# Another place in SBUF for the combined blocks, the activations and the raw weights, and a larger descriptor reserve for GpSimd's DMAs

## The chip, the cores and the metric

One Trainium2 chip, one core of it. The metric is the device time of one execution of the whole program in microseconds, as the median of several runs. TensorE, VectorE, ScalarE and GpSimd stand as PE, DVE, ACT and POOL in the profile; SyncE (SP) issues most of the DMAs, POOL issues some, and PEld is TensorE's weight load.

## What is computed

One decoder block on 1024 tokens of width 1024 in float32: half a SwiGLU feed forward, a mixer of two linear attentions with gates, half a SwiGLU feed forward, a final norm.

```python
def swiglu(h, w_gate, w_up, w_down):
    return (jax.nn.silu(h @ w_gate) * (h @ w_up)) @ w_down

h = h + FFN_RES * swiglu(rms_norm(h, ffn1_norm[layer]), ...)      # 1024 -> 2816 -> 1024
h = h + hybrid_mixer(rms_norm(h, mix_norm[layer]), ...)
h = h + FFN_RES * swiglu(rms_norm(h, ffn2_norm[layer]), ...)
return rms_norm(h, final_norm)
```

The mixer is a projection of h, gated linear attention with 4 heads, Gated DeltaNet with 8 heads in its chunked form (a triangular solve for each chunk of 64 tokens), gates on both, their sum, and an output projection.

## The kernel before

**Number format.** Every weight and activation of the large products is split into a high part and a low part (`wh`, `wl` for weights, `xh`, `xl` for activations). A product is three matmuls: `wh` with `xl`, `wl` with `xh`, `wh` with `xh`. Nearly all of them are 128x128 weights on 512 columns. A weight half arrives by an SP DMA in a tile `raw` (or `sr`), ACT casts it to `wh` (L119, L125) and DVE subtracts to get `wl` (L120, L126).

**Stages.** The first feed forward, the mixer, the second feed forward run one after the other. In a feed forward, gate and up projections are done for pairs of units by a Strassen scheme (`strassen`, matmuls at L367): seven products of 12 matmuls each. Four products read the split activations `xh`, `xl`; the other three read combined blocks of them, `t2h`, `t2l`, `t3h`, `t3l`, `t4h`, `t4l`, which are made once by `sums_own`. There are 20 such Strassen calls in each feed forward, that is 20 x 84 matmuls, 20 x 36 of them on combined blocks. The down projection (`down`, L573) uses the same six tiles anew, and `c11`, `c21`, `c22`, `wt`, for two of its four chunks, and `xn` tiles for the other two. The first and last rows of it go through `accumulate` (L138) with activations in `ah`, `al` and (last rows) in `t2h`, `t2l`; for the last rows the weights are kept in `t3h`, `t3l`, `t4h`, `t4l` by `hold`. The output projection of the mixer holds its second half of weights in the same way. The mixer has combined blocks of its own, from pool `mx`, for its Strassen calls (psum tag `m`).

**The triangular solves.** In the DeltaNet part, POOL inverts the blocks of one head while PE works on projections and on the head before. For each head POOL issues four DMAs of `em` to `l_d` (L920), four back to `lt` (L923), runs 31 pairs of multiply and subtract (L930, L933), then writes the result with four DMAs `x_d<-xp` of 1024 pieces each (L937) and one of `xt` (L938), and reads it back with eight DMAs to `xb` and `yb` (L949, L950). PE's first matmul on `xb` is at L986.

**Order.** The program is written in a tile language whose scheduler sets the order on each engine by priorities and its own view of when things are ready; each engine then runs its list in order. Tiles come from pools. A pool takes space from the low end of what is free, or from the high end with `side="right"`, when it is opened, and gives it back when it closes; a tile with a tag uses the slots of its tag in turn. The pools concerned:

```python
wp = ctx.enter_context(tc.tile_pool(name="wp", bufs=4))             # raw, wh, wl
...
raw = stage() if stage else wp.tile([P, 512], F32, name="raw", tag="raw", bufs=2)
...
hp = pool(st, "h1")       # the residual
tp = pool(st, "t1")       # everything else of the first feed forward
...
nc = _bacc.Bacc("TRN2", target_bir_lowering=False, num_devices=1, dynamic_dma_scratch_size=2048)
```

The last number is the bytes of each SBUF partition, from address 0, that are kept for the descriptors of DMAs which POOL issues.

Of the kernel before, what the change touches and what calls it, by code (L numbers as in the profile page):

```python
# [48 lines left out]
def tile_macaron_hybrid(  # L49
# [21 lines left out]
    xn = ctx.enter_context(tc.tile_pool(name="xn", bufs=1))  # L71
    wp = ctx.enter_context(tc.tile_pool(name="wp", bufs=4))

    nc.scalar.preload_act_table_set("sqrt_and_others")
# [234 lines left out]

    def strassen_products(tp, xs, tmp, corner, raws, place=bank, pool_steps=3):  # L310
        comb = {}
# [111 lines left out]

    def ffn(h, xs, wg, wu, wd, tp, ysc, first, last, pre, steps, after):
        def act_tiles():
            return [tp.tile([P, T], F32R, name=n, tag=n, bufs=2) for n in ("ah", "al")]

        def gate_up(j):
# [8 lines left out]
            if j == 0:  # L437
                b = tp.tile([P, T], F32, name="al", tag="al", bufs=2)
# [16 lines left out]
        def raws():  # L455
            return ([wp.tile([P, 512], F32, name="raw", tag="raw", bufs=2) for _ in range(2)] +
                    [stage() for _ in range(2)])
# [3 lines left out]

        sums_own, sums_inplace, strassen = strassen_products(tp, xs, weight_sum, weight_sum, raws, pool_steps=2)

# [61 lines left out]
        def chunk_ops(c):  # L525
            names = ("b11", "b21", "t2", "t3", "t1", "t4", "b22")
            res = {}
            for i, n in enumerate(names):
# [3 lines left out]
                elif i < 6:  # L532
                    m = ("t2h", "t2l", "t3h", "t3l", "t4h", "t4l")[i]
                    t = tp.tile([P, 4, 512], F32R, name=m, tag=m)
                    res[n] = [[t[:, 2 * p + k] for k in range(2)] for p in range(2)]
# [5 lines left out]
        def prepare(c, ops, first=None):  # L541
            parts = [first] if first else []
            for k in range(len(parts), 2):
                ss = [tp.tile([P, T], F32, name=n, tag=n, bufs=2) for n in (("ah", "al") if k and c else ("s", "s"))]
                for i in range(2):
# [5 lines left out]
        def down(u, ops, h0, h1, steps):  # L551
            r1 = wp.tile([P, 512], F32, name="raw", tag="raw", bufs=2)
            r2 = tp.tile([P, 512], F32, name="sr", tag="sr", bufs=2)
# [58 lines left out]
        with tc.issue_after(done[0]):  # L612
            at = [tp.tile([P, T], F32, name="ah", tag="ah", bufs=2) for _ in range(2)]
            for i in range(4):
                sums_inplace(i, lambda eng: at[i % 2][:, (LO, HI)[i // 2]])
# [22 lines left out]
        for n in ("t2h", "t2l"):  # L638
            t = tp.tile([P, 4, 512], F32R, name=n, tag=n).rearrange("p (j a) t -> p j (a t)", j=2)
            kept.append([t[:, k] for k in range(2)])  # L640
# [8 lines left out]
        ns = norm_space(tp)  # L649
        held = hold(wd, prev[0], tp)  # L650
        for seg in last:
# [9 lines left out]

    with ExitStack() as st:
        hp = pool(st, "h1")
        tp = pool(st, "t1")
# [25 lines left out]
        def between(seg, ns):  # L690
            steps = norm_steps(h, seg, P_MX, xs2, ns)
            if seg[0] == 0:
# [5 lines left out]
                       steps=steps)  # L698
        ffn(h, xs, g1, u1, d1, tp, ysc, FIRST, HALVES, begin1, None, between)
        with tc.high_priority(offset=-4000):  # L700
# [3 lines left out]
    with ExitStack() as st:  # L704
        with ExitStack() as stm:
            ys, h = mixer(stm, st, tc, pool, start, xs2, load_unit, dense, ptile, bank, rsqrt_newton, split, new_x,
                           accumulate, block_units(OBLOCKS), dram, pr, ident, ones, cst, eye, wlr, win,
                           wout, y_d, h_d, sqrt_table, strassen_products, wp, psum, divide, recent, pinned, run)
# [4 lines left out]
        held = hold(wout, units, tp)  # L713
        ysc = tp.tile([P, T], F32, name="ysc", tag="ysc")
# [18 lines left out]

        ffn(h, xs, g2, u2, d2, tp, ysc, HALVES, LAST, None, steps, finish)


def mixer(st, sto, tc, pool, start, xs, load_unit, dense, ptile, bank, rsqrt_newton, split, new_x, accumulate,
          ounits, dram, pr, ident, ones, cst, eye, wlr, win, wout, y_d, h_d, sqrt_table, strassen_products, wp, psum, divide, recent, pinned, run):
    nc = tc.nc
# [512 lines left out]
    for i in range(8):  # L1252
# [32 lines left out]
    sums_own, sums_inplace, strassen = strassen_products(  # L1285
        mx, xs, lambda: wp.tile([P, 512], F32, name="raw", tag="raw", bufs=2),
        lambda: wp.tile([P, 512], F32, name="raw", tag="raw", bufs=2),
        lambda: [mx.tile([P, 512], F32, name="sr", tag="sr", bufs=4) for _ in range(4)],
# [78 lines left out]
    sqrt_table()  # L1367
    return ys, h

# [85 lines left out]
```

## Time and profile before

| what | us |
|---|---|
| runs of the kernel | 2658.49, 2653.29, 2659.28 |
| median | 2658.49 |
| the profiled execution's own time | 2661.61 |
| its span, first to last instruction | 2659.8 |
| PE busy in the span | 2505.2 (94%) |
| DVE busy | 1872.5 (70%) |
| POOL busy | 1177.3 (44%) |
| ACT busy | 1069.3 (40%) |

Matmuls overlap each other in the records: a row gives the time from a matmul's start to its modelled end, and the next one starts before that. What a row of matmuls takes is read from the starts. The stages by the clock of the span: first feed forward 0 to 730 us (gate and up from 95 to 465, down to 671, last rows to 720), DeltaNet heads to about 1320, gated linear attention and gates to 1850, output projection to 1960, second feed forward to the end (gate and up from 2010 to 2390).

### The profile page before, as it was taken

How to read it: one execution, taken by the hardware profiler on the slowest of the kernel's cores; microseconds unless marked ns; L12 is line 12 of the kernel's file. 1: busy time of each engine (PE TensorE's matmuls, PEld its weight loads, DVE VectorE, ACT ScalarE, POOL GpSimd, SP SyncE). 2: the span in 40 equal slices, each digit the busy share in tenths (PEclk: the TensorE clock that was granted, in tenths of full speed). 3: DMA queues.
4: the chain of work that ended last, by engine and by line, in shares of the span. 5: the costliest groups of instructions: out<-in, count | busy, mean ns of one | idle time of the engine just before them, and what ended most of it. 6: DMA issues, size and time to landing. Idle time of an engine off the chain costs nothing.

```text
span 2659.8 us, 32713 instructions
## 1 busy us (share of the span) xinstructions
PE 2505.2 (94%) x11656; PEld 2020.1 (76%) x11656; DVE 1872.5 (70%) x2907; ACT 1069.3 (40%) x1847; POOL 1177.3 (44%) x1312
## 2 busy tenths in 40 slices
PE   7899999899986999999989999999989999998998
PEld 6788888667865777777767787878768888886677
DVE  8755555999685777886686766767586555558996
ACT  5333334333352444444354544535243333343331
POOL 4544444654227667776352222121154444446531
PEclk9999999999998999999999999999999999999999
DMA  3222221322221222212211212112312222213222
GB/s 116 76 68 88 87 87 58 117 80 84 106 84 48 60 64 60 60 44 56 60 55 40 84 36 84 60 60 91 119 32 80 76 79 84 91 60 112 80 87 79
DMA packets 93602, 199.03 MB, mean 75 GB/s; under 512 B 12248, under 2 KB 17112, under 8 KB 93440
## 3 DMA queue, kind: packets, MB, share of 16 engines
q1 hardware_dynamic: 82576, 175.64, 20.3%
q0 software_dynamic: 8704, 18.89, 2.7%
q10 hardware_dynamic: 2160, 2.43, 0.3%
q8 instruction: 91, 1.49, 0.2%
q14 instruction: 71, 0.58, 0.1%
HBM read 158.73 MB, written 38.17 MB: 74 GB/s over the span
## 4 chain that ended last, share of the span: by engine, by line
PE 66%; DVE 15%; POOL 5%; ACT 5%; issue 4%; DMA 2%; DVEq 0%; POOLq 0%; ACTq 0%
PE q L367 28%; PE ps L138 13%; PE m L367 10%; PE q L573 6%; DVE wl L126 2%; PE q L986 2%; DVE xl L126 1%; POOL itmp L930 1%; POOL xp L933 1%; DVE ha L578 1%; DVE h L578 1%; DMA s<-a_d 1%; ACT L803 1%; PE q L908 1%; DVE c L378 1%
## 5 line engine op out<-in xcount | busy, mean ns | idle before, releaser
L126 DVE TENSOR_TENSOR wl<-raw,wh 128x512 fp32r<-128x512 f32 x244 | 199.7, 819 | 173.1 <-ACT wh L125 171.6
L138 PE MATMUL ps<-xl,wh 128*128 128x512 f32 (+2 forms) x736 | 258.3, 410 | 22.9 <-ACT wh L119 8.0
L126 DVE TENSOR_TENSOR wl<-sr,wh 128x512 fp32r<-128x512 f32 x232 | 203.5, 878 | 78.6 <-ACT wh L125 78.2
L138 PE MATMUL ps<-xh,wh 128*128 128x512 f32 (+2 forms) x736 | 255.2, 406 | 0.0
L138 PE MATMUL ps<-xh,wl 128*128 128x512 f32 (+2 forms) x736 | 254.8, 404 | 0.1
L367 PE MATMUL q<-xl,wh 128*128 128x512 f32 x640 | 249.6, 390 | 0.3 <-ACT c L373 0.3
L367 PE MATMUL q<-xh,wl 128*128 128x512 f32 x640 | 249.7, 390 | 0.0
L367 PE MATMUL q<-xh,wh 128*128 128x512 f32 x640 | 249.6, 390 | 0.0
L125 ACT CAST wh<-sr 128x512 fp32r<-128x512 f32 x232 | 143.7, 619 | 243.4 <-PE q L573 61.8
L472 POOL TENSOR_TENSOR s<-s,ysc 128x512 f32<-128x512 f32 x80 | 112.5, 1417 | 247.2 <-ACT s L471 247.2
L125 ACT CAST wh<-raw 128x512 fp32r<-128x512 f32 x244 | 145.0, 594 | 176.5 <-PE q L367 98.3
L138 PEld LDWEIGHTS ps<-xl,wh 128*128 128x128 f32 (+1 forms) x736 | 138.8, 193 | 54.2 <-DVE xl L238 8.9
L355 POOL TENSOR_TENSOR raw<-sr 128x512 f32<-128x512 f32 x20 | 26.6, 1328 | 331.0 <-DMA sr<-in_win 269.8
L138 PEld LDWEIGHTS ps<-xh,wh 128*128 128x128 f32 (+1 forms) x736 | 138.7, 193 | 24.2 <-issue 1.0
L138 PEld LDWEIGHTS ps<-xh,wl 128*128 128x128 f32 (+1 forms) x736 | 138.9, 192 | 24.0 <-issue 0.9
L378 DVE TENSOR_TENSOR c<-c,q 128x512 f32<-128x512 f32 x120 | 82.4, 687 | 84.2 <-PE q L367 84.0
L367 PEld LDWEIGHTS q<-xl,wh 128*128 128x128 f32 x640 | 120.2, 188 | 26.8 <-issue 0.7
L367 PEld LDWEIGHTS q<-xh,wl 128*128 128x128 f32 x640 | 120.2, 188 | 25.5
L367 PEld LDWEIGHTS q<-xh,wh 128*128 128x128 f32 x640 | 120.2, 188 | 25.2
L373 ACT COPY c<-q 128x512 f32<-128x512 f32 x120 | 70.4, 587 | 162.2 <-PE q L367 161.8
L930 POOL TENSOR_TENSOR itmp<-lt,xp 128x112 f32<-128x112 f32 (+29 forms) x248 | 116.1, 468 | 36.1 <-DMA lt<-l_d 17.3
L933 POOL TENSOR_TENSOR xp<-xp,itmp 128x112 f32<-128x112 f32 (+29 forms) x248 | 120.0, 484 | 19.4
(490 smaller groups left out, 6848.7 us busy)
## 6 DMA issues: line engine op xcount, KB each, us to landing
sr<-in_win SPq DMA_DIRECT2D x80, 256.0 KB, 2.6
a_d<-s SPq DMA_DIRECT2D x36, 512.0 KB, 3.6
raw<-in_win SPq DMA_DIRECT2D x66, 256.0 KB, 2.6
raw<-in_d SPq DMA_DIRECT2D x56, 256.0 KB, 2.7
raw<-in_g SPq DMA_DIRECT2D x48, 256.0 KB, 2.6
s<-a_d SPq DMA_DIRECT2D x24, 512.0 KB, 4.1
sr<-in_u SPq DMA_DIRECT2D x44, 256.0 KB, 3.0
raw<-in_u SPq DMA_DIRECT2D x44, 256.0 KB, 2.6
```

Of the source, the lines that this page charges most:

```text
L125: a = nc.scalar.copy(out=hi, in_=src)
L126: b = (eng or nc.vector).tensor_sub(out=lo, in0=src, in1=hi.bitcast(F32))
L138: mm = nc.tensor.matmul(out=ps[:m, sl], lhsT=w[:, :m], rhs=x[:, sl], start=(i == 0 and a == 0), stop=(i == n - 1 and a == 2))
L367: nc.tensor.matmul(out=ps, lhsT=p[:, c], rhs=q, start=(first and k == 0 and a == 0), stop=(k == 3 and a == 2), skip_group_check=not first)
L373: marks[0] = nc.scalar.copy(out=t, in_=ps).ins
L378: marks[1] = nc.vector.tensor_add(out=t, in0=t, in1=ps).ins
L472: nc.gpsimd.tensor_mul(out=s, in0=s, in1=y)
L573: nc.tensor.matmul(out=ps, lhsT=p[:, c], rhs=q, start=(first and k == 0 and a == 0), stop=(k == 1 and a == 2), skip_group_check=not first)
L578: nc.vector.scalar_tensor_tensor(out=hd[:, sl], in0=ps, scalar=0.5, in1=hd[:, sl], op0=ALU.mult, op1=ALU.add)
L930: inv_eng.tensor_tensor(out=tv, in0=lp[:, j, j + 1:].unsqueeze(2).broadcast_to([P, r, m]), in1=xp[:, j, :m].unsqueeze(1).broadcast_to([P, ...
L933: inv_eng.tensor_tensor(out=xv, in0=xv, in1=tv, op=ALU.subtract)
L986: nc.tensor.matmul(out=q[:, c], lhsT=lhs[:, c], rhs=rhs[:, c], start=True, stop=True)
```

## The change

It is one edit in three parts. (1) A pool `rp` at the high end of SBUF holds the `raw` tiles, which were at the front of `wp`. (2) A pool `q1` (in the second feed forward `q2`) is opened ahead of the residual's pool and holds `t2h` to `t4l`, `ah` and `al`; the pool `t1` (`t2`) keeps the rest. (3) The reserve for POOL's DMAs grows from 2048 to 8192 bytes. No tile is added, none changes its size or its number of slots, and no instruction's work changes.

```diff
+    rp = ctx.enter_context(tc.tile_pool(name="rp", bufs=2, side="right"))
...
-            raw = stage() if stage else wp.tile([P, 512], F32, name="raw", tag="raw", bufs=2)
+            raw = stage() if stage else rp.tile([P, 512], F32, name="raw", tag="raw", bufs=2)
...
-    def strassen_products(tp, xs, tmp, corner, raws, place=bank, pool_steps=3):
+    def strassen_products(tp, xs, tmp, corner, raws, place=bank, pool_steps=3, tq=None):
...
-                comb[c] = [tp.tile([P, 4, 512], F32R, name=c + p, tag=c + p) for p in "hl"]
+                comb[c] = [(tq or tp).tile([P, 4, 512], F32R, name=c + p, tag=c + p) for p in "hl"]
...
-            return [tp.tile([P, T], F32R, name=n, tag=n, bufs=2) for n in ("ah", "al")]
+            return [tq.tile([P, T], F32R, name=n, tag=n, bufs=2) for n in ("ah", "al")]
...
-        held = hold(wd, prev[0], tp)
+        held = hold(wd, prev[0], tq)
...
     with ExitStack() as st:
+        tq = pool(st, "q1")
         hp = pool(st, "h1")
         tp = pool(st, "t1")
...
     stl.close()
+    tq = pool(sto, "q2")
     hp = pool(sto, "h2")
...
-    nc = _bacc.Bacc("TRN2", target_bir_lowering=False, num_devices=1, dynamic_dma_scratch_size=2048)
+    nc = _bacc.Bacc("TRN2", target_bir_lowering=False, num_devices=1, dynamic_dma_scratch_size=8192)
```

What lies where, in bytes from the start of a partition, as the built programs place it (a partition ends at 229,376):

| tiles | before | after |
|---|---|---|
| reserve for POOL's descriptors | 0 to 2,048 | 0 to 8,192 |
| `xh0` to `xl7` | 3,840 to 69,376 | 9,984 to 75,520 |
| `raw` | 69,376 to 73,472 | 225,248 to 229,344 |
| `wh`, `wl` | 73,472 to 89,856 | 75,520 to 91,904 |
| mixer's `t2h` to `t4l` (`mx`) | 89,856 to 139,008 | 91,904 to 141,056 |
| residual `h` | 89,856 to 122,624 | 157,440 to 190,208 |
| first feed forward: `t2h`, `t2l`, `t3h`, `t3l`, `t4h`, `t4l`, 8,192 each | 157,568 to 206,720 | 100,096 to 149,248 |
| second: `t3h`, `t3l`, `t4h`, `t4l` | 145,280 to 178,048 | 91,904 to 124,672 |
| second: `t2h`, `t2l` | 190,336 to 206,720 | 132,864 to 149,248 |
| `al` (two), first / second | 149,376 / 182,144, 8,192 long | 91,904 / 124,672 |
| `ah` (two), both | 206,720 to 214,912 | 149,248 to 157,440 |
| `s`, `sr`, `wt`, `c11` to `c22`, `ysc` | 122,624 to 149,248 or so | 190,208 to 216,832 or so |

**The order on the engines** is the same in both feed forwards and from about 1320 us on. It differs in the DeltaNet heads. Lines after L71 have moved by one to three, and buffer numbers differ. On PE, ahead of the first matmul on `xb` of the first head (`n` and `xb` are its inputs, `acc` the next values to be transposed, `ps` a projection), before:

```order
L138 MATMUL ps<-xl_5419,wh 128x512 x2
L138 MATMUL ps<-xh_5418,wl 128x512 x2
L138 MATMUL ps<-xh_5418,wh 128x512 x2
L138 MATMUL ps<-xl_5424,wh 128x512 x2
L138 MATMUL ps<-xh_5423,wl 128x512 x2
L986 MATMUL q<-xb,n_5770 128x128 x4
L138 MATMUL ps<-xh_5423,wh 128x512 x2
L138 MATMUL ps<-xl_5429,wh 128x512 x2
```

and with the change:

```order
L139 MATMUL ps<-xl_5425,wh 128x512 x2
L139 MATMUL ps<-xh_5424,wl 128x512 x2
L139 MATMUL ps<-xh_5424,wh 128x512 x2
L139 MATMUL ps<-xl_5430,wh 128x512 x2
L139 MATMUL ps<-xh_5429,wl 128x512 x2
L139 MATMUL ps<-xh_5429,wh 128x512 x2
L139 MATMUL ps<-xl_5435,wh 128x512
L989 MATMUL q<-xb,n_5777 128x128 x4
L139 MATMUL ps<-xl_5435,wh 128x512
```

Three projection matmuls that stood behind the matmul on `xb` now stand ahead of it (`xh_5423,wh` x2 and one of `xl_5429,wh`).

On PE again, some 60 us earlier: the transposes of the first head's keys (`q<-cs,kq`), those of the decay and beta rows (`q<-cs,yi`), and the first of the products of keys and queries (`q<-kq`), before:

```order
L1234 MATMUL q<-cs,yi 128x128
L138 MATMUL ps<-xl_5429,wh 128x512
L1234 MATMUL q<-cs,yi 128x128 x2
L882 MATMUL q<-cs,kq_5782 128x128 x8
L138 MATMUL ps<-xl_5429,wh 128x512
L138 MATMUL ps<-xh_5428,wl 128x512 x2
L138 MATMUL ps<-xh_5428,wh 128x512 x2
L138 MATMUL ps<-xl_5434,wh 128x512
L1234 MATMUL q<-cs,yi 128x128
```

and with the change:

```order
L139 MATMUL ps<-xl_5450,wh 128x512
L1237 MATMUL q<-cs,yi 128x128 x2
L885 MATMUL q<-cs,kq_5789 128x128 x2
L1237 MATMUL q<-cs,yi 128x128
L885 MATMUL q<-cs,kq_5789 128x128 x6
L1237 MATMUL q<-cs,yi 128x128
L139 MATMUL ps<-xl_5450,wh 128x512
L911 MATMUL q<-kq_5789 128x256 x4
```

The key transposes have moved back behind 18 projection matmuls and stand next to the `q<-kq` products, which stay at nearly the same place (three rows of projection later).

## Rows read from the trace of the kernel before

**Rows 1.** Windows by stage: stretch, length, busy us (instructions), granted clock, DMA share, GB/s.

```profile
core 0: us, PE busy (x) PEld busy (x) DVE busy (x) ACT busy (x) POOL busy (x), PEclk, DMA share, GB/s
...
320.00:440.00 120.00, 120.00 (x524) 98.08 (x523) 67.22 (x92) 45.43 (x79) 52.28 (x37) 1.00 0.23 73
...
520.00:600.00 80.00, 71.98 (x299) 54.56 (x298) 76.62 (x104) 29.65 (x55) 48.46 (x45) 1.00 0.23 73
...
800.00:860.00 60.00, 37.94 (x183) 30.84 (x181) 31.85 (x68) 11.59 (x21) 43.02 (x84) 0.83 0.19 50
860.00:925.00 65.00, 62.60 (x345) 50.03 (x344) 48.84 (x106) 27.87 (x54) 41.65 (x84) 1.00 0.23 64
...
2240.00:2360.00 120.00, 120.00 (x524) 98.16 (x523) 67.27 (x92) 44.69 (x77) 51.91 (x36) 1.00 0.25 82
```

**Rows 2.** Chain of work that ended last: start us, us, what.

```profile
95.12 369.59 PE q L367 x1608
...
2010.03 380.35 PE q L367 x1656
```

**Rows 3.** Timeline of PE, first feed forward: start us, us, engine line op tiles.

```profile
299.82 0.39 PE L367 MATMUL q<-xl,wh 128*128 128x512 f32 x1
...
301.86 0.40 PE L367 MATMUL q<-t2l,wh 128*128 128x512 f32 x1
...
304.65 0.40 PE L367 MATMUL q<-t3l,wh 128*128 128x512 f32 x1
```

**Rows 4.** Timeline of PE, mixer, 24 matmuls on its combined blocks.

```profile
1601.19 0.39 PE L367 MATMUL m<-t2l,wh 128*128 128x512 f32 x1
...
1603.91 0.39 PE L367 MATMUL m<-t3l,wh 128*128 128x512 f32 x1
...
1606.63 0.39 PE L367 MATMUL m<-xl,wh 128*128 128x512 f32 x1
```

**Rows 5.** PE by shape: 96 to 464, 672 to 693, 1895 to 1930 us (busy us, mean ns).

```profile
L367 PE MATMUL q<-xh,wh 128*128 128x512 f32 x307 | 119.7, 390 | 0.0
...
L367 PE MATMUL q<-t3h,wh 128*128 128x512 f32 x76 | 30.0, 395 | 0.0
...
L138 PE MATMUL ps<-ah,t3h 128*128 128x512 f32 x8 | 2.5, 389 | 0.0
...
L138 PE MATMUL ps<-xh,t3h 128*128 128x512 f32 x32 | 10.0, 395 | 0.0
...
L138 PE MATMUL ps<-xh,wh 128*128 128x512 f32 x10 | 3.1, 390 | 0.0
```

**Rows 6.** PE's waits, 500 to 640 us: total, times, longest.

```profile
PE q L573 <- DVE ha L578: 12.9, 14, 2.6
```

**Rows 7.** Timeline of POOL, first head; in brackets the idle time before.

```profile
831.32 0.83 POOL L937 DMA_DIRECT2D x_d<-xp  x1
834.37 0.78 POOL L937 DMA_DIRECT2D x_d<-xp  x1 [2.21 <-issue]
837.25 0.77 POOL L937 DMA_DIRECT2D x_d<-xp  x1 [2.10 <-issue]
840.12 0.78 POOL L937 DMA_DIRECT2D x_d<-xp  x1 [2.10 <-issue]
...
843.33 0.58 POOL L949 DMA_DIRECT2D xb<-x_d  x1 [0.70 <-DMA x_d<-xp]
```

**Rows 8.** POOL's waits, whole span, and DMA issues of the page's view: KB, us to landing.

```profile
POOL x_d L937 <- issue: 60.1, 24, 4.3
...
x_d<-xp POOLq DMA_DIRECT2D x32, 32.0 KB, 2.6
```

**Rows 9.** PE's waits, 730 to 1320 us.

```profile
PE q L986 <- DMA xb<-x_d: 25.6, 4, 20.9
PE q L908 <- DVE h L805: 6.7, 6, 1.3
```

**Rows 10.** Casts and subtractions of weights by tile read, whole span (512 columns).

```profile
L125 ACT CAST wh<-raw 128x512 fp32r<-128x512 f32 x212 | 131.9, 622 | 157.4 <-PE q L367 98.3 <-PE q L573 39.0 <-PE ps L138 7.4
...
L125 ACT CAST wh<-sr 128x512 fp32r<-128x512 f32 x232 | 143.7, 619 | 243.4 <-PE q L573 61.8 <-PE q L367 60.0 <-PE m L367 44.5
```

More of the change, by code (lines that the diff above doesn't have):

```diff
@@ L422, in strassen_products, with ffn @@
         return sums_own, sums_inplace, strassen
-    def ffn(h, xs, wg, wu, wd, tp, ysc, first, last, pre, steps, after):
+    def ffn(h, xs, wg, wu, wd, tq, tp, ysc, first, last, pre, steps, after):
         def act_tiles():
-            return [tp.tile([P, T], F32R, name=n, tag=n, bufs=2) for n in ("ah", "al")]
+            return [tq.tile([P, T], F32R, name=n, tag=n, bufs=2) for n in ("ah", "al")]
         def gate_up(j):
@@ L437, in gate_up @@
             if j == 0:
-                b = tp.tile([P, T], F32, name="al", tag="al", bufs=2)
+                b = tq.tile([P, T], F32, name="al", tag="al", bufs=2)
                 with tc.high_priority(offset=400):
@@ L455, in raws @@
         def raws():
-            return ([wp.tile([P, 512], F32, name="raw", tag="raw", bufs=2) for _ in range(2)] +
+            return ([rp.tile([P, 512], F32, name="raw", tag="raw", bufs=2) for _ in range(2)] +
                     [stage() for _ in range(2)])
@@ L460, in weight_sum @@
             return tp.tile([P, 512], F32, name="wt", tag="wt", bufs=2)
-        sums_own, sums_inplace, strassen = strassen_products(tp, xs, weight_sum, weight_sum, raws, pool_steps=2)
+        sums_own, sums_inplace, strassen = strassen_products(tp, xs, weight_sum, weight_sum, raws, pool_steps=2, tq=tq)
         def gate_up2(j):
@@ L533, in chunk_ops @@
                     m = ("t2h", "t2l", "t3h", "t3l", "t4h", "t4l")[i]
-                    t = tp.tile([P, 4, 512], F32R, name=m, tag=m)
+                    t = tq.tile([P, 4, 512], F32R, name=m, tag=m)
                     res[n] = [[t[:, 2 * p + k] for k in range(2)] for p in range(2)]
@@ L543, in prepare @@
             for k in range(len(parts), 2):
-                ss = [tp.tile([P, T], F32, name=n, tag=n, bufs=2) for n in (("ah", "al") if k and c else ("s", "s"))]
+                ss = [p.tile([P, T], F32, name=n, tag=n, bufs=2)
+                      for p, n in (((tq, "ah"), (tq, "al")) if k and c else ((tp, "s"), (tp, "s")))]
                 for i in range(2):
@@ L551, in down @@
         def down(u, ops, h0, h1, steps):
-            r1 = wp.tile([P, 512], F32, name="raw", tag="raw", bufs=2)
+            r1 = rp.tile([P, 512], F32, name="raw", tag="raw", bufs=2)
             r2 = tp.tile([P, 512], F32, name="sr", tag="sr", bufs=2)
@@ L612, in ffn @@
         with tc.issue_after(done[0]):
-            at = [tp.tile([P, T], F32, name="ah", tag="ah", bufs=2) for _ in range(2)]
+            at = [tq.tile([P, T], F32, name="ah", tag="ah", bufs=2) for _ in range(2)]
             for i in range(4):
@@ L638, in ffn @@
         for n in ("t2h", "t2l"):
-            t = tp.tile([P, 4, 512], F32R, name=n, tag=n).rearrange("p (j a) t -> p j (a t)", j=2)
+            t = tq.tile([P, 4, 512], F32R, name=n, tag=n).rearrange("p (j a) t -> p j (a t)", j=2)
             kept.append([t[:, k] for k in range(2)])
@@ L698, in between @@
                        steps=steps)
-        ffn(h, xs, g1, u1, d1, tp, ysc, FIRST, HALVES, begin1, None, between)
+        ffn(h, xs, g1, u1, d1, tq, tp, ysc, FIRST, HALVES, begin1, None, between)
         with tc.high_priority(offset=-4000):
@@ L705, in tile_macaron_hybrid @@
         with ExitStack() as stm:
-            ys, h = mixer(stm, st, tc, pool, start, xs2, load_unit, dense, ptile, bank, rsqrt_newton, split, new_x,
+            ys, h, tq = mixer(stm, st, tc, pool, start, xs2, load_unit, dense, ptile, bank, rsqrt_newton, split, new_x,
                            accumulate, block_units(OBLOCKS), dram, pr, ident, ones, cst, eye, wlr, win,
-                           wout, y_d, h_d, sqrt_table, strassen_products, wp, psum, divide, recent, pinned, run)
+                           wout, y_d, h_d, sqrt_table, strassen_products, rp, psum, divide, recent, pinned, run)
         tp = pool(st, "t2")
@@ L712, in tile_macaron_hybrid @@
         units = block_units(OBLOCKS)[1]
-        held = hold(wout, units, tp)
+        held = hold(wout, units, tq)
         ysc = tp.tile([P, T], F32, name="ysc", tag="ysc")
@@ L732, in finish @@
                 (nc.sync if k % 2 else nc.scalar).dma_start(out=out[k, :, sl], in_=o)
[L734 removed]
+        ffn(h, xs, g2, u2, d2, tq, tp, ysc, HALVES, LAST, None, steps, finish)
 def mixer(st, sto, tc, pool, start, xs, load_unit, dense, ptile, bank, rsqrt_newton, split, new_x, accumulate,
[L738 removed]
+          ounits, dram, pr, ident, ones, cst, eye, wlr, win, wout, y_d, h_d, sqrt_table, strassen_products, rp, psum, divide, recent, pinned, run):
     nc = tc.nc
@@ L1285, in mixer @@
     sums_own, sums_inplace, strassen = strassen_products(
-        mx, xs, lambda: wp.tile([P, 512], F32, name="raw", tag="raw", bufs=2),
-        lambda: wp.tile([P, 512], F32, name="raw", tag="raw", bufs=2),
+        mx, xs, lambda: rp.tile([P, 512], F32, name="raw", tag="raw", bufs=2),
+        lambda: rp.tile([P, 512], F32, name="raw", tag="raw", bufs=2),
         lambda: [mx.tile([P, 512], F32, name="sr", tag="sr", bufs=4) for _ in range(4)],
@@ L1367, in mixer @@
     sqrt_table()
-    return ys, h
+    return ys, h, tq
 def _units(w):
```

## The prediction

> **What bounds the kernel now.** I read the windows by stage first. In the gate and up stage of both feed forwards PE is busy for 120.00 of 120 us while DVE has 67 and ACT 45 [rows 1], so there the time is the number of matmuls times the distance of their starts, and nothing else. The chain of waits says the same: one unbroken piece of 369.59 us in the first and of 380.35 us in the second [rows 2]. The down stage is shared: DVE is busy for 76.6 of 80 us and PE for 72 [rows 1], and PE waits for DVE 14 times, 12.9 us in all [rows 6]. In the DeltaNet heads PE is nearly full (62.6 of 65 us) except ahead of the first head's inverse, where it has 37.9 of 60 us [rows 1]. PE's waits there name the transfer to `xb`: 25.6 us in four waits, the longest 20.9 [rows 9]. That transfer ends a chain through POOL.
>
> **The cadence of matmuls depends on where both operands lie.** The chain has 229.85 ns a matmul in the first feed forward (369.59/1608) [rows 2], and it is not one cadence but two. On `xh`, `xl` nine matmuls take 301.86 - 299.82 = 2.04 us, 226.7 ns each; on the combined blocks twelve take 304.65 - 301.86 = 2.79 us, 232.5 ns each [rows 3]. The share fits: 36 of 84 matmuls at 5.8 ns more make 2.5 ns on the mean, most of the 3.15 between 226.7 and 229.85. What sets the two apart? Not the tiles' role: the mixer's combined blocks, 24 matmuls, take 1606.63 - 1601.19 = 5.44 us, 226.7 ns each [rows 4]. In the mixer they lie at 89,856 to 139,008, in the feed forwards at 145,280 and above, with the weights `wh`, `wl` below 90,000 in both. Nor is a high address slow by itself: `ah` with weights held in `t3h`, both high, has 389 ns; `xh` low with `t3h` high has 395; `xh` with `wh`, both low, has 390 [rows 5]. So a matmul costs about 5 ns more when its two operands lie on opposite sides of an address between 139,008 and 145,280. The change puts nearly all operands on the low side.
>
> **Part 1, the combined blocks and activations.** Gate and up: 720 matmuls on combined blocks in each feed forward, 1440 in all, have operands on both sides now. After, `t2h` to `t4h` end at 141,056 or below. One low-part tile (`t4l` in the first, `t2l` in the second) lies at 141,056 to 149,248; I count it as far, and it is in 80 of 720 matmuls. So 1440 - 160 = 1280 matmuls gain 5.8 ns [rows 3, 4]: **-7.4 us**. All of it is on the path, since PE does not wait there [rows 1, 2]; the next engine, DVE, has 53 us of slack in 120. Down: of about 640 crossed matmuls some 190 stay crossed (those on `c11`, `c22`, `wt` and the one far tile); 450 x 5 ns = 2.3 us, of which I take half, as DVE is as full as PE there [rows 1, 6]: **-1.1 us**. Held output projection: 192 matmuls of `xh`, `xl` with weights in `t3h` to `t4l` go from 395 to 390 [rows 5]: **-1.0 us**. Rows of `accumulate` with `ah`, `al`: first rows gain 64 of 192 matmuls, 0.3 us; last rows had both operands high and now cross where `ah` meets held weights, and in the first feed forward where `t4l` is held, some 220 matmuls x 5 ns = 1.1 us: together **+0.8 us**. Sum of the placement: **-8.7 us**. Bounds: 0 if the address is not the cause, -11 if every crossed matmul counted here came down and the down stage passed all of it on.
>
> [...] The rows have 226.7 against 232.5 ns with no other engine changing at the border, so I go by the rows.
>
> **Part 2, the raw weights.** They are read by ACT and DVE (and POOL) alone, and written by DMAs. ACT's cast takes 622 ns from `raw` at 69 to 73 thousand and 619 ns from `sr`, which lies at 127,000 to 153,000 [rows 10]. A reader's distance costs nothing there, so I take 0, between bounds of -3 and +3 ns for 300 casts that are mostly hidden, +-0.5 us.
>
> **Part 3, the reserve.** For each head POOL sends `x_d<-xp` in four DMAs of 1024 pieces. It issues one in 0.8 us and then stands idle for 2.1 us before the next one, with nothing that the profile shows to wait for [rows 7]. A start comes every 2.9 to 3.1 us, and such a DMA lands 2.6 us after its issue [rows 8]: each is let go just after the one before has landed. That is what a full descriptor reserve would look like, and no other POOL DMA has this spacing. All 24 gaps, three for each head, are 60.1 us [rows 8]. With four times the room I expect the four in a row. First head: issues at 831.3, 832.2, 832.9 and 833.7 in place of 831.3 to 840.1, so the last lands 6.4 us earlier; three L138 matmuls now ahead of the wait add 0.7 us of useful work, and the `q<-kq` products that start the chain come three matmuls, 0.7 us, later, which cancels it. PE's wait of 20.9 us becomes about 14.5 [rows 9]: **-6 us**, allowing 0.4 us for four DMAs that share the engines. Later heads: the other three waits for `xb`, 25.6 - 20.9 = 4.7 us [rows 9], are each shorter than the 6.4 us that POOL gains and vanish: **-4.5 us**, with 0.2 us left for order. What is late next there is DVE: PE already waits 6.7 us in six waits for the step ahead of `q<-kq` [rows 9]. The rest of the 60 us lies beside PE's work. Sum: **-10.5 us**. Bounds: 0 if the gaps have another cause, -15 if POOL's lead also shortens some of those waits for DVE.
>
> [...]
>
> **The order.** In the heads the scheduler's list changes by a few matmuls here and there. The key transposes come 18 matmuls (4.1 us) later, but what they lead to is needed only beside the `q<-kq` products; I take 0 with bounds of -2 and +3 us.
>
> **The sum.** -8.7 + 0 - 10.5 + 0 = -19.2 us. Against the profiled execution's own time, 2661.6 (its span 2659.8 and 1.8 around it), that gives 2642.4. The median of the runs is 2658.5, 3.1 below the profiled one; the saving is in stages that do not differ between runs, so the forecast for the median is 2658.5 - 19.2 = **2639.3 us**, 0.7% faster.
>
> **The rivals.**
> (a) The reserve works, the placement doesn't: the cadence of 232.5 ns comes with the feed forward's combined blocks for a reason other than their address. For it: no other stage has the same tile at both kinds of address. Against it: the three pairs in rows 5, where role and address part. -10.5 us: 2648.
> (b) The placement works, the gaps stay: POOL's pause is its own work on 1024 pieces, not room. For it: the cause isn't named in the rows. Against it: the pause is as long as the landing, and the issue itself is over in 0.8 us. -8.7 us: 2649.8.
> (c) Both work, and the heads give most of it back: POOL is early, but the new order makes DVE or ACT late at `acc` and `q<-kq`, a microsecond or two for each of eight heads, 8 to 14 us: 2650 to 2653, within 0.3% of before.
> (d) Slower. The four DMAs of each head, no longer spaced, sit together on the 16 DMA engines in front of the `raw` weights that SP fetches for the projections. A raw half feeds 24 matmuls, 24 x 0.227 = 5.4 us, and two halves are in store, so a load of 2.6 us can be about 5 to 8 us late before PE stands. To end 0.3% above before, the eight heads must lose 8 + 19 = 27 us, 3.4 us each: a load would have to be some 10 us late. The four DMAs today take 2.6 us each, 10.4 us if they were served one by one ahead of a load. From there on it decides: 2667 or more. Against it: DMA share is 0.23 in these windows [rows 1].
>
> **How the numbers follow.** Both work as summed: 0.68. (a) 0.09, (b) 0.08, (c) 0.11, (d) 0.04. About 0.3%, 8 us here, is what a measurement of this kernel can tell from no change. Faster by more than that (below 2650.5) are the forecast, (a), and two thirds of (b): 0.68 + 0.09 + 0.05 = 0.82, and a bit of (c): 0.83. Within 0.3%: the rest of (b) and nearly all of (c), 0.13. Slower 0.04. The range: downwards both lower bounds are -11 and -15, and half of the way from -19.2 to -26 and order's -2 give 2633; with the spread of runs (they lie within 6 us of each other) 2632. Upwards it takes in (a) and (b): 2650.5.
>
> **What would show it.** Step by step in the trace after: combined blocks of the feed forwards at 390 ns by shape instead of 395, with one low-part tile still near 395; the gate and up pieces of the chain shorter by some 3.7 us each; `x_d<-xp` issues 0.8 us apart and no waits at L937's line; the longest wait for `xb` near 14 to 15 us and the others gone; 390 in the held output projection and 395 in the last rows where `ah` meets held weights. The prediction is wrong if the combined blocks stay at 395, if the gaps stay at 2 us, or if both go and PE's waits for DVE in the heads grow by what was saved.

## The result and the profile after

The changed kernel takes **2629.80 us** (median of four runs, 2625.72 to 2630.56) against 2655.89 for the kernel before in the runs beside it (2651.91 to 2659.28). The ratio is **0.9892, 95% interval 0.9876 to 0.9908**: 29 us faster, between 24 and 33; the two medians lie 26 us apart. Forecast was 2639.3, a gain of 19.2 us, so the sign was right and 7 to 9.5 us of gain were not seen coming; the time lies 2.2 us below the lower end of the range, which was 2632. A second set of runs of the changed kernel gave 2627.95 against 2655.82, ratio 0.9894 (0.9879 to 0.9909).

The work is the same: the page of the kernel after (engine, busy us, instructions) has as many matmuls as before, 11656. The span is 31.7 us shorter; PE is busy for 14.3 us less, and the rest is idle time that is gone.

```profile
PE 2490.9 (95%) x11656; PEld 2018.1 (77%) x11656; DVE 1877.5 (71%) x2907; ACT 1069.3 (41%) x1847; POOL 1175.8 (45%) x1312
```

**Feed forwards.** The two long pieces of the chain of the kernel after (start, us, what; line L368 is L367 of before) are 4.8 and 5.0 us shorter than in [rows 2]:

```profile
95.33 364.77 PE q L368 x1608
...
1984.64 375.37 PE q L368 x1656
```

By shape (instructions | busy us, mean ns of one), every combined block stands at the 389 ns of `xh`, where [rows 5] had 395. That holds for `t4l` too, which was forecast to stay dear; of the group, 320 to 440 us:

```profile
L368 PE MATMUL q<-xh,wh 128*128 128x512 f32 x99 | 38.5, 389 | 0.0
...
L368 PE MATMUL q<-t3h,wh 128*128 128x512 f32 x28 | 10.9, 389 | 0.0
...
L368 PE MATMUL q<-t4l,wh 128*128 128x512 f32 x24 | 9.3, 389 | 0.0
```

**Heads.** POOL's timeline of the first head shows the four DMAs of [rows 7] as one piece of 3.17 us without a gap (they took 9.6), and the wait for the landing behind it:

```profile
824.12 3.17 POOL L940 DMA_DIRECT2D x_d<-xp  x4
827.24 0.60 POOL L941 DMA_DIRECT2D x_d<-xt  x1
830.03 0.59 POOL L952 DMA_DIRECT2D xb<-x_d  x1 [1.03 <-DMA x_d<-xp]
```

PE's waits (total, times, longest), 727 to 1300 us, have one wait for `xb` of 13.4 us in place of four with 25.6 [rows 9]; the waits for DVE ahead of `q<-kq`, which might have grown, are 6.9 for 6.7:

```profile
PE q L989 <- DMA xb<-x_d: 13.4, 1, 13.4
PE q L911 <- DVE h L808: 6.9, 6, 1.3
```

**Where the gain is.** I read from the traces when each stage's first matmul starts, and list the distances in us, one column for each kernel's profiled execution. That of before took 2661.6 us, more than its medians (2655 to 2658.5), so the distances add up to more than the medians give. The kernels in the middle are the experiments below. "Mixer's products" are its Strassen calls and the linear attention; "output, first" is the output projection up to the first matmul with held weights, "output, held" is the rest up to the second feed forward's products; the last row ends ahead of the last rows of the down projection.

| stage | before | reserve (e1) | grid (e3) | both (e9) | placement (e2) | third order (e10) | h2 low (e6) | after | after again (e11) |
|---|---|---|---|---|---|---|---|---|---|
| gate and up, 1st | 422.3 | 422.2 | 418.0 | 417.9 | 417.9 | 418.0 | 417.9 | 419.0 | 417.4 |
| down and last rows, 1st | 195.9 | 195.7 | 194.8 | 194.3 | 195.2 | 194.1 | 197.4 | 194.3 | 195.1 |
| norm to first `q<-kq` | 77.4 | 77.4 | 77.4 | 77.4 | 76.0 | 77.3 | 75.9 | 76.0 | 76.0 |
| to first `xb` | 78.5 | 72.8 | 78.6 | 72.4 | 77.7 | 72.1 | 71.7 | 71.8 | 72.3 |
| heads | 521.5 | 516.2 | 522.2 | 515.7 | 519.0 | 515.8 | 514.4 | 513.6 | 514.3 |
| mixer's products | 482.4 | 477.1 | 480.5 | 482.7 | 479.1 | 477.1 | 480.4 | 482.7 | 478.7 |
| output, first | 48.1 | 47.5 | 47.7 | 47.8 | 43.7 | 43.7 | 47.7 | 43.7 | 43.7 |
| output, held | 109.1 | 109.1 | 108.4 | 108.5 | 108.4 | 108.4 | 108.4 | 108.5 | 108.5 |
| gate and up, 2nd | 413.1 | 412.7 | 408.3 | 408.4 | 408.3 | 408.4 | 408.4 | 407.7 | 408.3 |
| down, 2nd | 175.9 | 174.5 | 174.3 | 174.4 | 174.4 | 173.6 | 176.5 | 174.9 | 173.0 |

Against before, the last two columns have 9 to 10 us from gate and up, 2 to 4 from the down stages, 15 to 16 from the norm to the end of the heads (three rows), 4.3 from the first part of the output projection and 0.6 from its held part. The mixer's products vary by 5.6 us among kernels that do not differ there; the last section has the granted clock that goes with it.

### The profile page after: what moved, and what is told of

Its sections match the earlier page's. It is cut to its first block, busy times and chain, and to the rows that moved or that the text cites. A ratio compares the mean times of both kernels' runs of the same rounds, so it can differ in the third digit from the quotient of the medians.

```text
span 2628.1 us, 32714 instructions
## 1 busy us (share of the span) xinstructions
PE 2490.9 (95%) x11656; PEld 2018.1 (77%) x11656; DVE 1877.5 (71%) x2907; ACT 1069.3 (41%) x1847; POOL 1175.8 (45%) x1312
## 4 chain that ended last, share of the span: by engine, by line
PE 69%; DVE 14%; ACT 5%; issue 4%; POOL 3%; DMA 2%; DVEq 0%; POOLq 0%; ACTq 0%
PE q L368 28%; PE ps L139 15%; PE m L368 10%; PE q L575 6%; DVE wl L127 3%; PE q L989 2%; DVE h L580 1%; DVE xl L127 1%; DVE ha L580 1%; PE q L911 1%; DMA s<-a_d 1%; ACT L806 1%; PE q L1002 1%; PE q L1026 1%; POOL xp L936 1%
## 5 line engine op out<-in xcount | busy, mean ns | idle before, releaser
L127 DVE TENSOR_TENSOR wl<-raw,wh 128x512 fp32r<-128x512 f32 x244 | 209.3, 858 | 167.3 <-ACT wh L126 165.9
L368 PE MATMUL q<-xl,wh 128*128 128x512 f32 x640 | 249.0, 389 | 0.5 <-ACT c L374 0.5
L368 PE MATMUL q<-xh,wh 128*128 128x512 f32 x640 | 249.0, 389 | 0.0
L368 PE MATMUL q<-xh,wl 128*128 128x512 f32 x640 | 249.0, 389 | 0.0
L368 PEld LDWEIGHTS q<-xl,wh 128*128 128x128 f32 x640 | 120.1, 188 | 25.8 <-issue 0.9
L368 PEld LDWEIGHTS q<-xh,wh 128*128 128x128 f32 x640 | 120.1, 188 | 25.0
L368 PEld LDWEIGHTS q<-xh,wl 128*128 128x128 f32 x640 | 120.1, 188 | 24.9
```

Source lines behind the costliest of these rows:

```text
L127: b = (eng or nc.vector).tensor_sub(out=lo, in0=src, in1=hi.bitcast(F32))
L368: nc.tensor.matmul(out=ps, lhsT=p[:, c], rhs=q, start=(first and k == 0 and a == 0), stop=(k == 3 and a == 2), skip_group_check=not first)
```

## The experiments

Ratios are against the kernel before in runs on the same chip, with 95% intervals.

**e1: the reserve alone.**

```diff
-    nc = _bacc.Bacc(..., dynamic_dma_scratch_size=2048)
+    nc = _bacc.Bacc(..., dynamic_dma_scratch_size=8192)
```

> The kernel before with the scratch of dynamic DMAs at 8192 bytes and nothing else; every tile moves up by 6144 bytes, all together, so the distances between tiles stay. Theory R (POOL stood at a full descriptor reserve): the starts of x_d<-xp come 0.8 us apart, the heads gain the 14.6 us that the changed kernel gained there, with 1.4 us ahead of the first head, about 16 us or 0.6% in all; the feed forwards keep 232.5 ns on their combined blocks and gain nothing; the output projection keeps its late h. Prediction's own figure for this part was 10.5 us. Rival: part of the heads' gain came from the placement (other tiles in other places, another order), then this run gains clearly less than 14 us in the heads.

Measured: 2642.66, ratio 0.9957 (0.9942 to 0.9972), 11.4 us. Every engine's list of instructions is that of before. POOL's timeline of the first head:

```profile
830.99 3.17 POOL L937 DMA_DIRECT2D x_d<-xp  x4
834.11 0.59 POOL L938 DMA_DIRECT2D x_d<-xt  x1
836.90 0.59 POOL L949 DMA_DIRECT2D xb<-x_d  x1 [1.03 <-DMA x_d<-xp]
```

and PE's wait for `xb`, 740 to 845 us:

```profile
PE q L986 <- DMA xb<-x_d: 14.8, 1, 14.8
```

The gaps are gone by the reserve alone, and it is worth 5.7 us up to the first `xb` and 5.3 behind it, 11.0 in all. That is the prediction's 10.5, not the 16 that I expected after seeing the changed kernel: the rest of what the heads gained there is not the reserve's.

**e2: the placement alone.** The changed kernel with the scratch at 2048 bytes.

> The changed kernel with the scratch back at 2048 bytes: the placement alone. Theory: gaps of 2.1 us between the x_d<-xp starts are back and the heads stand as before; the feed forwards have 226.7 ns on all blocks, 4.6 + 5.4 us in gate and up and about 1 us in the second down stage; the output projection gains 4.9 us because the h loads no longer wait for the mixer's t2h. Sum about 15.7 us, 0.6% below before. Rival: the output projection's gain comes from the reserve (eight h<-h_d DMAs that POOL issues in a row), then the sum here is about 11 us and e1 has the other 5.

Measured: 2637.51, ratio 0.9936 (0.9923 to 0.9949), 17.0 us. POOL's gaps are back and PE's wait for `xb` is 19.0 (all engines' waits, 738 to 843 us):

```profile
PE q L989 <- DMA xb<-x_d: 19.0, 1, 19.0
...
POOL x_d L940 <- issue: 6.4, 3, 2.2
```

The two parts add up: 0.43% and 0.64% make 1.07%, the whole change has 1.08%. The placement is worth twice the forecast 8.7. The table shows what the prediction lacked: 4.3 us in the first part of the output projection, and 4.6 us from the norm to the end of the heads (1.4 + 0.8 + 2.4, before rounding), where gaps and reserve are as before.

**e3: on the grid, no pool moved.** The grid stands here for the addresses at multiples of 256 bytes (e4 shows why 256). The six pairs of combined blocks stay high, 1,920 bytes above their place in the kernel before; only the four small tiles ahead of them grow.

```diff
-        nv, ny = ([tp.tile([P, 8], F32, ...) for _ in range(2)] for n in ("nv", "ny"))
+        nv, ny = ([tp.tile([P, 128], F32, ...)[:, :8] for _ in range(2)] for n in ("nv", "ny"))
```

> The kernel before with one edit: the four small tiles nv, ny of 32 bytes, which stand ahead of the combined blocks in t1 and t2, take 512 bytes each. So the blocks stay high (147,200 to 216,832), 1920 bytes further up than before, but their addresses no longer differ by 128 from those of x and w in a grid of 2048 bytes. Theory of the prediction (a border, or the distance of the two operands): the blocks stay at 232.5 ns and the time does not change (within 1 us). Rival G (the grid: a matmul costs 5 to 6 ns more when its two operands stand at different places in the grid): all blocks at 226.7 ns, x with held weights 390 in place of 395, time 10 to 11 us (0.4%) below before.

Measured: 2647.41, ratio 0.9974 (0.9964 to 0.9985), 6.9 us. The blocks lie at 147,200 to 208,640, further from the weights than before, and yet (PE by shape, 320 to 440 us):

```profile
L367 PE MATMUL q<-xh,wh 128*128 128x512 f32 x99 | 38.5, 389 | 0.0
...
L367 PE MATMUL q<-t3h,wh 128*128 128x512 f32 x28 | 10.9, 389 | 0.0
...
L367 PE MATMUL q<-t4h,wh 128*128 128x512 f32 x24 | 9.3, 389 | 0.0
```

So the border that the prediction put between 139,008 and 145,280 does not exist. Gate and up gain 4.3 and 4.7 us, the same as with the whole placement. The 6.9 us of the ratio are less than the 10 to 11 of rival G. The twelve runs of e3 have a lower granted clock than the 17 of before beside them (mean 0.981 against 0.984), and among the 38 runs of before in all sessions 0.001 less of it goes with 1.4 us more; by an estimate from these figures some 4 us of the gain are hidden by that. What had made the blocks dear is 128 bytes: `x`, `wh`, `wl` and the mixer's blocks stood at multiples of 256 (3,840; 73,472; 89,856), the feed forwards' blocks 128 behind one (157,568; 145,280), pushed there by four tiles of 32 bytes. [rows 5] had this all along: `ah` and `t3h`, 128 off both, go well together (389 ns), `xh` and `t3h` do not (395).

**e4: off the grid by different amounts.** The changed kernel with unused pads, so that one kernel tries six offsets. The numbers count elements of 4 bytes; the first group is for the first feed forward, and pads add up along the pool.

```diff
+    shift = [{"t2h": 8, "t3h": 8, "t4h": 16}, {"t3h": 64, "t4h": 64, "t2h": 128}]
...
+    def pad(tq, n):
+        if tq and n in shift[0]:
+            tq.tile([P, shift[0].pop(n)], F32, name="z" + n, tag="z" + n)
...
+                pad(tq, c + "h")
```

> The changed kernel with unused pads ahead of some tiles, so that blocks stand off the grid of x and w by a different amount each: in the first feed forward t2 by 32 bytes, t3 by 64, t4 and ah by 128, al by 0; in the second t3 by 256, t4 by 512, t2 and ah by 1024, al by 0. Theory of the prediction (border or distance): 226.7 ns on all, time as the changed kernel. Rival G: the blocks that stand off the grid go to 232 ns, those off by a multiple of its period stay at 226.7; if all six differ, 10 to 11 us above the changed kernel, and which of the sizes are dear gives the period.

Measured: 2633.01, ratio 0.9916 (0.9901 to 0.9931). By shape, 320 to 440 us, with `t2h` 32 bytes off, `t3h` 64, `t4h` 128:

```profile
L378 PE MATMUL q<-xh,wh 128*128 128x512 f32 x98 | 38.1, 389 | 0.0
...
L378 PE MATMUL q<-t2h,wh 128*128 128x512 f32 x28 | 11.1, 396 | 0.0
...
L378 PE MATMUL q<-t3h,wh 128*128 128x512 f32 x25 | 9.8, 394 | 0.0
...
L378 PE MATMUL q<-t3l,wh 128*128 128x512 f32 x25 | 9.8, 391 | 0.0
L378 PE MATMUL q<-t4h,wh 128*128 128x512 f32 x24 | 9.5, 395 | 0.0
```

and 2200 to 2320 us, with `t2h` off by 1024, `t3h` by 256, `t4h` by 512:

```profile
L378 PE MATMUL q<-t2h,wh 128*128 128x512 f32 x28 | 10.9, 389 | 0.0
...
L378 PE MATMUL q<-t3h,wh 128*128 128x512 f32 x28 | 10.9, 389 | 0.0
...
L378 PE MATMUL q<-t4h,wh 128*128 128x512 f32 x24 | 9.3, 389 | 0.0
```

32, 64 and 128 bytes are dear (391 to 396 ns), 256, 512 and 1024 are not (389): the grid has 256 bytes. The first feed forward's gate and up are back at 421.9 us, the second's stay at 408.4, and the median is 3 to 5 us above the changed kernel's two. The blocks here lie low, where the prediction called them near.

**e5: ha low again, the blocks high.**

```diff
-        tq = pool(st, "q1")
         hp = pool(st, "h1")
+        tq = pool(st, "q1")
```

> The changed kernel with the pool h1 opened ahead of q1, so that ha lies at 91,904 again, under the mixer's tiles n1, xb, yb, kq0, as in the kernel before; the combined blocks of the first feed forward move up to 124,672 and above, on the grid. Every engine's order of instructions is that of the changed kernel. The placement alone moved the start of the heads by 1.4 us and the heads by 3.2 us. Theory O (the new order of matmuls did that): both stay, time as the changed kernel. Rival H (the mixer's first tiles no longer wait for the stores of ha): the 4.6 us come back, 2634.5. By the grid the first feed forward keeps 226.7 ns everywhere; by a border some blocks, now at 160,000 to 190,000, would go to 232.

Measured: 2627.84, ratio 0.9892 (0.9875 to 0.9910). From the norm to the end of the heads it takes 661.1 us, the changed kernel 661.3 and 662.6. So it is not the stores of `ha` that held up the mixer; theory O stands so far, by exclusion only. Blocks at 132,864 to 182,016 have 389 ns.

**e6: h2 low again.**

```diff
-    tq = pool(sto, "q2")
     hp = pool(sto, "h2")
+    tq = pool(sto, "q2")
```

> The changed kernel with the pool h2 opened ahead of q2: h0 to h7 lie at 91,904 to 124,672 again, under the mixer's combined blocks as in the kernel before, and the second feed forward's blocks at 124,672 to 190,208. Order unchanged. Theory: the eight h loads wait again for the last readers of the mixer's blocks, PE stands again some 4 us in the output projection, and the time is 4.2 us above the changed kernel, 2634; blocks stay at 226.7 ns. Rival: the output projection's 4.2 us came from the order, then nothing comes back.

Measured: 2635.37, ratio 0.9920 (0.9900 to 0.9940). The first part of the output projection takes 47.7 us again (43.7 in the changed kernel), with every engine's list unchanged. What is late there is `h`, the residual that POOL loads back into `h0` to `h7`. In the kernel before POOL sends the eight loads together (start, us, idle time ahead), and PE and DVE then wait for them (1850 to 1905 us):

```profile
1860.81 4.43 POOL L1365 DMA_DIRECT2D h<-h_d  x8 [27.01 <-DVE xl L126]
```

```profile
PE ps L138 <- DVE h L281: 3.0, 1, 3.0
DVE h L281 <- DMA h<-h_d: 2.8, 1, 2.8
```

In the kernel after three of them go at once and five after a wait:

```profile
1813.14 1.68 POOL L1369 DMA_DIRECT2D h<-h_d  x3
1835.00 0.54 POOL L1369 DMA_DIRECT2D h<-h_d  x1 [20.18 <-ACT xh L126]
1835.92 2.12 POOL L1369 DMA_DIRECT2D h<-h_d  x4 [0.39 <-issue]
```

and in e6 all eight wait again:

```profile
1840.63 2.22 POOL L1369 DMA_DIRECT2D h<-h_d  x4 [26.79 <-DVE xl L127]
1843.09 2.13 POOL L1369 DMA_DIRECT2D h<-h_d  x4 [0.24 <-issue]
```

Low, `h0` and `h1` lie under the mixer's `t2h`, which is used once more, at the very end, as the place from which the fifth and sixth of the eight `y` tiles are split; POOL's first load waits for that, and the other seven stand behind it. High, the eight lie on places that are read for the first four splits at the latest: POOL's first three loads have nothing to wait for and go some 27 us sooner, the other five some 7 us sooner, counted from the end of POOL's work before the loads. Of this 4 us reach PE. The median is 6 to 7 us above the changed kernel; the 4.0 us of the stage are shown, the rest lies in the spread of runs (the first down stage has 197.4 here, where the other kernels have 194.1 to 195.9).

**e7 and, beside the changed kernel, e12: raw back beside the weights.**

```diff
-    rp = ctx.enter_context(tc.tile_pool(name="rp", bufs=2, side="right"))
+    rp = wp
```

> The changed kernel with raw back in the pool of the weights, at 75,520, so part 2 alone undone; order unchanged, all on the grid. Theory (a place on the grid costs no reader anything): same time as the changed kernel within 1 us, casts of raw at 620 ns in both. Rival: raw beside the weights disturbs the matmuls, then cadence and time rise.

> The changed kernel itself once more, beside the next one on the same chip: 2625 to 2631.

> Part 2 alone undone once more (raw back beside the weights), now beside the changed kernel on the same chip. In the first comparison it came out 4.7 us below the changed kernel's median, from another session. Theory (raw's place costs nothing): the two medians within 2 us, casts of raw at 620 ns in both. Rival (raw at the far end costs its readers or the matmuls something): the changed kernel again 3 to 5 us above.

Measured: e7 2625.06, ratio 0.9884 (0.9864 to 0.9904). That is below the changed kernel, so I ran the two side by side: e11, the changed kernel, 2627.95, ratio 0.9894 (0.9879 to 0.9909); e12 2627.68, ratio 0.9896 (0.9879 to 0.9913). The first difference was that of two sessions. Casts by shape in e12:

```profile
L126 ACT CAST wh<-sr 128x512 fp32r<-128x512 f32 x232 | 143.6, 620 | 244.7 <-PE q L368 59.8 <-PE q L575 53.0 <-PE m L368 44.9
L126 ACT CAST wh<-raw 128x512 fp32r<-128x512 f32 x212 | 131.9, 622 | 155.2 <-PE q L368 95.3 <-PE q L575 37.9 <-PE ps L139 10.7
```

and the same cast of `raw` in the changed kernel, from the far end of SBUF:

```profile
L126 ACT CAST wh<-raw 128x512 fp32r<-128x512 f32 x212 | 131.7, 621 | 153.4 <-PE q L368 95.4 <-PE q L575 38.0 <-PE ps L139 8.8
```

Part 2 is worth nothing, as forecast.

**e8: a reserve of 4096 bytes.** The changed kernel with `dynamic_dma_scratch_size=4096`.

> The changed kernel with a reserve of 4096 bytes. If the reserve is a ring of descriptors, one x_d<-xp takes more than half of 2048 bytes and at most all of it, so 4096 hold two or three: the first two or three starts 0.8 us apart, the one after them late by 0.5 to 1.3 us, the wait for xb 13.9 to 15 us in place of 13.4, and nearly all of the heads' gain kept, time 2630 to 2633. If the gain had another cause than room (the reserve's place, say), the gaps would be all there or all gone.

Measured: 2628.33, ratio 0.9897 (0.9880 to 0.9913). POOL's timeline, first head:

```profile
823.07 2.40 POOL L940 DMA_DIRECT2D x_d<-xp  x3
826.11 0.78 POOL L940 DMA_DIRECT2D x_d<-xp  x1 [0.63 <-issue]
829.29 0.58 POOL L952 DMA_DIRECT2D xb<-x_d  x1 [0.68 <-DMA x_d<-xp]
```

Three in a row, then one gap of 0.63 us: room is what counts, with one in a row at 2048 bytes [rows 7] and four at 8192 (e1). By an estimate from these counts, if nothing else holds room in the reserve at that time, a DMA of 1024 pieces takes over 1024 and at most 1365 bytes (four don't fit in 4096, three do). The gap costs nothing that can be measured: PE's wait for `xb` is 14.8 us, as in e7 and e11, which have no gap.

**e9: the reserve and the grid, no pool moved.** The edits of e1 and e3 in the kernel before.

> The kernel before with two edits, the reserve of 8192 bytes and nv, ny at 512 bytes each (the blocks on the grid, where they were): no pool moved, every engine's order that of the kernel before. Sum of the two apart: 0.43% and 0.26%, some 18 us, 2637. Against the changed kernel there lack then the output projection's 4 us and what the new order gave in the heads, 3 to 5 us. If this run comes to the changed kernel's time, order and h loads are worth nothing.

Measured: 2634.78, ratio 0.9913 (0.9897 to 0.9930), 23 us. Two lines give four fifths of the gain. That is more than the 18 us expected from the ratios of e1 and e3; e3's had its lower clock in it. Lacking are the 4 us of the output projection and 2 to 4 us in the heads.

**e10: a third order.** The changed kernel with `q1` opened behind `t1`, and e3's edit to keep it on the grid.

> The changed kernel with q1 opened behind t1, and nv, ny at 512 bytes so that q1 stays on the grid: every cost named so far is as in the changed kernel (226.7 ns, reserve, h2 away from the mixer's blocks), but the scheduler writes a third order of the heads (214 rows of PE's list differ from the changed kernel's, 127 from before's). Theory O: the heads and their start differ from the changed kernel's by microseconds either way, the feed forwards and the output projection by less than 1 us. If the heads take the changed kernel's time within 1 us, the order is worth little and the 4.6 us of the heads need another cause.

Measured: 2629.23, ratio 0.9895 (0.9880 to 0.9910). From the norm to the end of the heads it takes 665.2 us, as e9 with the order of before (665.5), against 661.3 and 662.6 in the changed kernel's order (661.1 to 663.2 in the eight executions that have it: after, e4 to e8, e11, e12); all other stages are those of the changed kernel. Reserve, grid and addresses of the mixer's tiles are the same here, the list is not. That speaks for theory O but does not isolate it. No run changes the list alone: `t1` lies low in before, e9 and e10 and high in the eight, so the mixer's first tiles also take the places of other tiles, the kind of thing that e6 priced for `h`. The traces speak against this rival: from 690 to 860 us in before, e9, e10, e2, e5 and after, no wait over 0.15 us ahead of a line of the mixer is put down to an instruction of the first feed forward or its norm. So the order is the likeliest cause. Windows over this stretch (length, busy us, clock) of the kernel before, of e2 (placement, changed order) and of e9 (reserve, order of before) show that PE works as long in each, within 2 us, and that only its idle time shrinks:

```profile
693.00:1370.00 677.00, 619.35 (x3256) 492.61 (x3255) 497.75 (x1012) 281.09 (x517) 397.48 (x719) 0.98 0.21 61
```

```profile
688.00:1361.00 673.00, 619.72 (x3259) 493.32 (x3258) 498.15 (x1013) 281.50 (x518) 398.22 (x720) 0.98 0.21 61
```

```profile
687.00:1353.00 666.00, 621.25 (x3260) 494.57 (x3259) 500.19 (x1013) 281.46 (x518) 396.60 (x720) 0.98 0.22 62
```

The three idle for 57.7, 53.3 and 44.8 us. In e2 the waits for `xb` sum to 22.5 in place of 25.6, the rest of the 4.4 us comes in pieces of a few tenths. e10's median is nevertheless the changed kernel's: its 3 us in the heads are within the spread. Which single moved matmul gives the 4 us was not tried.

## Why the prediction was right and wrong

**Right.** The reserve: 10.5 us forecast, 11.0 (e1) by stages and 11.4 by the ratio; 6 for the first head against 5.7, 4.5 for the others against 5.3. The gaps were a full reserve: 4, 3 and 1 of the DMAs go in a row at 8192 (e1), 4096 (e8) and 2048 bytes [rows 7]. What one of them puts there no run shows; the counts give only the estimate beside e8. Part 2 at nothing: e12. What bounds each stage: gate and up became shorter by all that the matmuls saved, since PE never waits there (busy for 120.00 of 120 us before, and after in the same stretch, 320 to 440 us).

**Rivals.** (a) and (b) fall, both parts work alone. (c) falls: nothing in the heads was given back. (d) falls: PE's only long wait stays the one for `xb`, and no load of weights is among its waits in the heads.

**Wrong in the cause, nearly right in the size by luck.** The step "a matmul costs about 5 ns more when its two operands lie on opposite sides of an address" failed. The three rows that it rested on fit a border and fit the 256-byte grid, and the prediction took the coarse reading without looking at the low bits of the addresses, which the layout gives. e3 decides it, and e4 shows the reverse, low blocks off the grid that are dear. On the matmuls the placement paid because the new pools happened to put every block on the grid, and that is why the forecast size came out near. The error cost these terms: 160 gate and up matmuls and some 190 of the down stage were counted as staying dear, and 0.8 us were charged for new crossings of `ah`. All came down: gate and up 8.4 by 1440 x 5.8 and 9.0 by stages (e3: 4.3 + 4.7) for 7.4 forecast, down stages and last rows 2.7 (e3: 1.1 + 1.6) for 0.3, the held projection 0.7 for 1.0. Together 12.4 by stages for 8.7, or 10.4 against the column of e1, which has the same list as before. e3's ratio gives 6.9, with 9.6 as the end of its interval; with the 4 us estimated above for the clock it comes near the stages. The down stages, which differ by 3 us among kernels that agree there, are the least sure. The prediction's bound of -11 for this part was also short of its own counts: 1440 x 5.8, 640 x 5 and 192 x 5 ns make 12.5 us. That the prediction went by its rows was right all the same: no other engine's work differs between before and e3, and 389 against 395 ns stand in one trace for the same tile name (`t4h` in e4).

**The order, counted as 0.** The prediction saw a few matmuls moved, priced one move at 0 and bounded the whole with -2 and +3 us. The stretch gains 4.6 us with the placement (e2), and 2 to 4 with the reserve as well (e9 and e10 against the changed kernel); the order is the likeliest cause, by e5 and e10, but not isolated. The bound of -2 was too tight: with 58 us of PE's idle time in this stretch there is room for more than 2.

**Not in the sum at all.** The residual `h0` to `h7` moved with the pools, from under the mixer's last-read blocks to a place that is free sooner: 4.3 us by the stage, of which e6 takes back 4.0. The prediction followed the moved tiles as operands of matmuls and never asked, of each moved tile, whose place it takes and when that place comes free.

The bookkeeping: forecast 19.2, measured 26 by the medians and 29 by the ratio. Beyond the forecast the grid's terms have 2 to 4 us, the stretch of the order 2 to 4, the loads of `h` 4.3, the reserve 0.5 to 1. That is 9 to 13 for a gap of 7 to 9.5; the interval of the ratio is 4 us wide on either side. The range missed because its lower end went only half of the way to the prediction's own bounds (its terms make 2633.9, where it says 2633); the full bounds, -26 and -2, would have given 2630.5, still 0.7 above the time. Of the gap between the forecast 2639.3 and 2629.8, 2.6 us are the kernel before, which had 2658.5 on record and 2655.9 beside the changed kernel.

## What to carry to other kernels

Before moving tiles for speed, look at their addresses modulo 256: here four tiles of 32 bytes ahead of the blocks made 1440 matmuls 2.5% dearer (232.5 ns for 226.7), and padding them was one line. Of every tile that a change of pools moves, ask two things apart: what reading it costs at the new place, and what the new place was used for last, since its first write waited for that here (26.8 us of POOL and 4.0 us of the stage for `h` in e6). Where a queue's DMAs come at the distance of one landing, with nothing to wait for (here a start every 2.9 to 3.1 us and 2.6 us to landing), try a larger reserve, and one in between to see whether room is what counts.

## What the runs showed of the hardware

**The grid of 256 bytes.** A matmul of 128x512 in float32r took 389 to 390 ns here (starts 226.7 apart [rows 3, 4]) when moving operand and weights stand at the same place modulo 256, and 391 to 396 when they are 32, 64 or 128 bytes apart (e4; starts 232.5 apart at 128 [rows 3]). It is the difference that counts: both 128 off has 389 [rows 5]. Other sizes and types of operand were not tried.

**The clock in the mixer's products.** Before and e1 have the same list of instructions and PE the same waits in this stage (10 us for `c` ahead of L1095, 4 for ACT, 4 for `h`, in both), and e1 is 5.3 us faster in it. Windows of 40 us at the same place of the program, first before, then e1 (PE busy 37.80 in both, then the granted clock):

```profile
1490.00:1530.00 40.00, 37.80 (x166) 30.22 (x165) 24.02 (x35) 16.30 (x29) 11.46 (x8) 0.96 0.23 75
```

```profile
1479.00:1519.00 40.00, 37.80 (x172) 30.26 (x171) 23.84 (x31) 16.50 (x30) 11.51 (x8) 1.00 0.23 73
```

PE stands for 0.41 and 1.79 us there in both. In before (start, us, tiles, idle time ahead) the matmuls after it start 427 ns apart for some 3 us (granted clock 0.54 to 0.61 of full speed from 1504 to 1508 us):

```profile
1504.80 1.12 PE L1095 MATMUL q<-cs,c 128*128 128x128 f32 x4 [1.79 <-DVE c L378]
1505.57 0.78 PE L367 MATMUL m<-t2h,wl 128*128 128x512 f32 x1
1506.14 0.63 PE L367 MATMUL m<-t2h,wh 128*128 128x512 f32 x1
1506.57 0.63 PE L367 MATMUL m<-t2l,wh 128*128 128x512 f32 x1
```

In e1 they start 228 ns apart there, at a granted clock of 1.00:

```profile
1492.94 0.66 PE L1095 MATMUL q<-cs,c 128*128 128x128 f32 x4 [1.79 <-DVE c L378]
1493.35 0.48 PE L367 MATMUL m<-t2h,wl 128*128 128x512 f32 x1
1493.67 0.40 PE L367 MATMUL m<-t2h,wh 128*128 128x512 f32 x1
1493.90 0.39 PE L367 MATMUL m<-t2l,wh 128*128 128x512 f32 x1
```

Before has three such windows at 0.96 in this stage, e1 none: 5.3 us, 1.8 for each; e2 has one and 479.1 us, e3 two and 480.5. So behind the same idle time of 1.8 us before lost another 1.8 us and e1 none. The granted clock goes with a good part of the spread among runs of one kernel: four runs of e1 have 2638.6 to 2643.2 us at granted clocks of 0.987 and 0.988, two have 2647.4 and 2649.4 at 0.983 and 0.982. So e1's ratio may hold some of this, its 11.0 us by stages do not, and this stage was left out of the account.
